# A transformer block on one core: order of the first columns, of the route and of the last experts' end

## The chip, the cores and the metric

The kernel runs on one core of a Trainium2 chip. The metric is device time in microseconds (us) of one execution; a kernel is compared by the median of several runs. The profile is that of one execution.

## The reference, cut to what matters

One block of a network on 256 tokens of width 2048, in float32:

```python
mod = silu(c) @ w_ada + b_ada                       # six vectors of 2048
sh1, sc1, gt1, sh2, sc2, gt2 = split(mod, 6)
h = rmsnorm(x, g_norm1) * (1 + sc1) + sh1
parts = split_cols(h @ w_in)                        # 10312 columns
y_att = dsa_attention(...)                          # indexer, top 64 keys, 8 heads
y_hg  = rmsnorm(hgrn2_recurrence(...), g_head) * silu(hog)
merged = sigmoid(ga) * (y_att @ w_attn_up) + sigmoid(gh) * (y_hg @ w_hgrn_up)
x = x + gt1 * (merged @ w_out)
h2 = rmsnorm(x, g_norm2) * (1 + sc2) + sh2
x = x + gt2 * hier_moe(h2, ...)                     # 4 groups of 8 experts, 2 experts a token
out = rmsnorm(x, g_final)
```

Each expert has a gate, an up (2048 x 512) and a down matrix (512 x 2048).

## The kernel before

**Stages.** Tokens lie in two tiles of 128 rows (t = 0, 1); the width is cut into KT = 16 slices j of 128. The stages run in the order of `Block.__init__`: `prepare`, `first_columns`, `middle_columns`, `merge`, `project` (which ends in `route`), `experts`, `overflow` (a branch that this input doesn't take) and `finish`.

**Weights.** All weights come over the SP queue. `unit` loads a piece of a dense matrix, `ada` a row block of w_ada (128 x 2048, 1 MB), both into a ring of RING = 5 slots of 1 MB. A ring slot is free again when its last reader is done, so SP waits at the first load whose slot isn't free, and everything behind it on that queue waits too.

**First columns.** The dense products up to w_out are made exact enough by splitting: `split_w` has ACT round a weight piece of two slices j to fp32r (`hi`, L249) and DVE subtract it (`lo`, L250), and `three` multiplies hi, lo and the low part of the left side in three matmuls (L273 to L275). `first_columns` takes the 16 slices in five groups (2, 3, 4, 4, 3 slices) and each group through 11 column blocks (9 of 512, 2 of 292). A group needs its normalized features (`features`: two ACT operations and one DVE subtraction per slice j), which need the two `ada` sums per slice, each one DVE instruction over 128 x 2048 (L388). In the first four groups the order on each engine is that of the program (`manual_schedule`): for a column block, its splits and matmuls (`column`), then the addition of the column block before (`add`: ACT copies in the first group, DVE adds later), then `ada` sums for the next group, and at the last column block `features` of the next group. `first_norm` makes the row norms and transposes x by 32 matmuls against a diagonal (eight pieces of four, each with one ACT copy, L348 and L350); `early` (the first sums and features) stands after the first two pieces. The fifth group and all until `project`'s end are ordered by the planner. `lower_bounds` and `router_weights`, called there, load small tensors over SP; the planner sends these loads far ahead.

**Project and route.** `tokens_out` adds the gate times the product to x, sums squares (ACT, L1018), transposes x on PE (L1021) and multiplies by the router weights (L1010). For the last quarter this and `route` stand in an order written out: `spread_rows` makes 128 equal rows of a quarter of the last gate by four matmuls (L431), `rows` copies them (L986). Then come the logits (L1050), the choice of experts on DVE, the positions by three matmuls (L1082 to L1084), `tokens_high` (ACT, L1030) and `tokens_low` (DVE, L1036).

**Experts.** 32 experts in pairs. `block(e, u)` multiplies one quarter of gate and up of expert e (2 MB of weights, L1185), with the tokens gathered by `gather` (L1367, L1370) four experts at a time; `hidden` makes silu(gate) * up; `down` multiplies a quarter of the down matrices of the pair (2 MB, L1293), scales by weight and gate (L1296), splits (L1298, L1299); `scatter` adds it to the tokens (L1380, L1381). The weights go through the order `ring_order`: 5 ring slots of 1 MB, one slot of 1 MB of tag t8 and R2 = 3 slots of 2 MB (`ring2`, whose memory is that of the closed dense pool). `slot` loads 1 MB (L1133), `two` 2 MB (L1144), or halves of a quarter (L1135, L1147).

**End.** At the last pair, `prepare_finish` takes two of the ring slots for the result (`zg`), resets the order to two ring slots and three of 2 MB, and makes the rows of g_final: per quarter four DVE scalings of the identity (L1389), one matmul (L1391) and two ACT copies (L1404). The last quarter of the down product is cut in two halves of 256 columns, each with loads of its own. `scale_columns` sums squares (L1413) and multiplies by g_final (L1416); `finish` makes the row factors (L1424 on), scales (L1429, L1430) and stores by eight DMAs (L1432).

## Time and profile before

| | |
|---|---|
| median of 3 runs | 1787.6 us (1783.95 to 1790.62) |
| profiled execution, its time | 1786.46 us |
| its span, first to last instruction | 1784.5 us |
| PE busy, DVE busy, ACT busy | 91%, 52%, 29% of the span |
| moved by DMA | 631.32 MB, mean 354 GB/s |

Spans are sums over stages with different limits, so the rows below are read stage by stage. In a row of a timeline the first number is the start, the second the duration or, for a merged row, the time from the first to the last end; the brackets give the idle time of that engine before it and what ended it. SPq is the queue on which SP issues DMAs; a number there is issue time, not transfer.

### The profile page before, as it was taken

Reading aid. Unit: us, or ns where it says so; the run is one execution under the profiler, and the core shown is the slowest. Engines: PE = TensorE matmul, PEld = TensorE weight load, DVE = VectorE, ACT = ScalarE, POOL = GpSimd, SP = SyncE. Lnnn points to the kernel's source line nnn. Section 1 sums busy time; section 2 is a strip of 40 time slices with the busy share of each in tenths; the row PEclk is TensorE's granted clock in tenths of the full one; section 3 lists DMA queues with packets and bytes.
Section 4 is the critical chain, followed back from the end, with each engine's and each line's share of the span. In section 5 each row is a group of like instructions: output and inputs, shape, how many; then the busy total and the mean of one; then the engine's idle time right before and its main releaser. Section 6 shows DMA issues by size and latency. Waiting matters only on the chain. (4 is left out here: it accounts for less than half of the span.)

```text
span 1784.5 us, 19070 instructions
## 1 busy us (share of the span) xinstructions
PE 1629.3 (91%) x7453; PEld 962.0 (54%) x7453; DVE 928.6 (52%) x1517; ACT 523.4 (29%) x876; POOL 8.5 (0%) x19
## 2 busy tenths in 40 slices
PE   4889998899999999999999998988989989889885
PEld 4667786577777888885343433433424334234232
DVE  5789798998788799763321222122212221232125
ACT  4533446365654444434020110200201102002003
POOL 0000000000000000000000000000000000000000
PEclk9999998899999999998999999999999999999998
DMA  8888765578667989887999999999999999999994
GB/s 309 304 329 325 254 232 187 218 262 310 260 239 294 342 328 353 333 300 322 423 425 424 425 424 425 423 426 424 424 424 425 424 424 423 425 424 425 424 409 179
DMA packets 82942, 631.32 MB, mean 354 GB/s; under 512 B 13120, under 2 KB 15456, under 8 KB 21920
## 3 DMA queue, kind: packets, MB, share of 16 engines
q1 hardware_dynamic: 81728, 627.04, 87.9%
q0 software_dynamic: 944, 2.94, 0.6%
q8 instruction: 61, 1.00, 0.2%
q14 instruction: 33, 0.27, 0.0%
q10 hardware_dynamic: 176, 0.07, 0.0%
HBM read 627.92 MB, written 2.10 MB: 353 GB/s over the span
## 5 line engine op out<-in xcount | busy, mean ns | idle before, releaser
L1185 PE MATMUL moe_acc<-moe_u,moe_xg 128*64 128x512 f32 x2048 | 479.4, 601 | 51.6 <-DMA moe_u<-w_exp_in 51.6
L1185 PEld LDWEIGHTS moe_acc<-moe_u,moe_xg 128*64 128x64 f32 x2048 | 153.7, 137 | 325.7 <-issue 248.0
L1293 PE MATMUL moe_acc<-moe_u,moe_hT 128*64 128x512 f32 (+1 forms) x1040 | 233.0, 590 | 18.4 <-DMA moe_u<-w_exp_down 17.7
L1246 DVE COPY moe_gu<-moe_acc 128x512 f32<-128x512 f32 x32 | 22.1, 691 | 330.3 <-PE moe_acc L1185 330.3
L1293 PEld LDWEIGHTS moe_acc<-moe_u,moe_hT 128*64 128x64 f32 x1040 | 81.1, 137 | 153.1 <-issue 136.0
L1296 DVE SCALAR_TENSOR_TENSOR moe_ys<-moe_acc,moe_cw,out_t 128x512 f32<-128x512 f32 (+1 forms) x65 | 48.3, 743 | 177.7 <-PE moe_acc L1293 177.6
L1298 ACT ACTIVATE moe_yp<-moe_ys 128x512 fp32r<-128x512 f32 (+1 forms) x65 | 40.5, 623 | 307.1 <-DVE moe_ys L1296 307.1
L274 PE MATMUL first_acc<-first_wl,first_t 128*128 128x512 f32 (+1 forms) x292 | 115.5, 395 | 13.3 <-DVE first_wl L250 13.1
L273 PE MATMUL first_acc<-first_wr,first_t 128*128 128x512 f32 (+1 forms) x292 | 113.8, 390 | 7.4 <-ACT first_wr L249 7.4
L275 PE MATMUL first_acc<-first_wr,first_t 128*128 128x512 f32 (+1 forms) x292 | 113.1, 387 | 0.0
L273 PE MATMUL gate_acc<-gate_wr,first_t 128*128 128x512 f32 x256 | 103.9, 407 | 0.7 <-ACT gate_wr L249 0.7
L249 ACT ACTIVATE first_wr<-first_u 128x1024 fp32r<-128x1024 f32 (+3 forms) x79 | 73.1, 932 | 101.8 <-PE first_acc L275 89.0
L274 PE MATMUL gate_acc<-gate_wl,first_t 128*128 128x512 f32 x256 | 102.4, 400 | 0.1
L275 PE MATMUL gate_acc<-gate_wr,first_t 128*128 128x512 f32 x256 | 102.1, 399 | 0.0
L1381 DVE TENSOR_TENSOR out_t<-out_t,moe_ps 128x512 f32<-128x512 f32 (+1 forms) x130 | 82.1, 673 | 31.9 <-PE moe_ps L1380 31.9
L250 DVE TENSOR_TENSOR first_wl<-first_u,first_wr 128x1024 fp32r<-128x1024 f32 (+3 forms) x79 | 81.9, 1067 | 25.8 <-ACT first_wr L249 25.6
L1257 ACT ACTIVATE moe_si<-moe_ps 128x256 f32<-128x256 f32 x32 | 12.4, 387 | 281.3 <-PE moe_ps L1254 281.3
L249 ACT ACTIVATE gate_wr<-gate_u 128x1024 fp32r<-128x1024 f32 x64 | 67.8, 1059 | 77.8 <-PE gate_acc L275 65.0
L250 DVE TENSOR_TENSOR gate_wl<-gate_u,gate_wr 128x1024 fp32r<-128x1024 f32 x64 | 77.7, 1221 | 18.2 <-ACT gate_wr L249 18.0
L1370 ACT ACTIVATE moe_xg<-moe_ps,pre_c,pre_c 128x256 f32<-128x256 f32 x128 | 63.7, 565 | 65.2 <-PE moe_ps L1367 64.5
L1380 PE MATMUL moe_ps<-moe_yp,moe_S 128*128 128x512 f32 (+1 forms) x260 | 77.8, 421 | 2.8 <-ACT moe_yp L1298 2.8
L1380 PEld LDWEIGHTS moe_ps<-moe_yp,moe_S 128*128 128x128 f32 x260 | 43.8, 188 | 60.3 <-issue 49.9
(366 smaller groups left out, 2359.1 us busy)
## 6 DMA issues: line engine op xcount, KB each, us to landing
moe_u<-w_exp_in SPq DMA_DIRECT2D x160, 1024.0 KB, 23.7
moe_u<-w_exp_in SPq DMA_DIRECT2D x48, 2048.0 KB, 24.7
moe_u<-w_exp_down SPq DMA_DIRECT2D x47, 2048.0 KB, 24.6
first_u<-w_ada SPq DMA_DIRECT2D x32, 1024.0 KB, 7.1
gate_u<-w_in SPq DMA_DIRECT2D x32, 1024.0 KB, 5.7
moe_u<-w_exp_down SPq DMA_DIRECT2D x32, 1024.0 KB, 24.2
gate_u<-w_ada SPq DMA_DIRECT2D x28, 1024.0 KB, 4.9
first_u<-w_in SPq DMA_DIRECT2D x18, 1024.0 KB, 7.0
```

Source lines behind the costliest of these rows:

```text
L249: nc.scalar.activation(hi, raw, AF.Copy)
L250: nc.vector.tensor_sub(lo, raw, hi.bitcast(F32))
L273: mm(out, lr, hi, start=start, stop=False)
L274: mm(out, lr, lo, start=False, stop=False)
L275: mm(out, ll, hi, start=False, stop=stop)
L1185: nc.tensor.matmul(gu[e][64 * k:64 * k + 64, :], xg[g][j][:, CAP * i:CAP * i + CAP], w[k][:, jj, :], start=j == 0, stop=j == KT - 1, skip_ ...
L1293: nc.tensor.matmul(yp[64 * i:64 * i + 64, :n], h[i][:, f, :], w[i][:, f, :], start=f == 0, stop=f == 3, skip_group_check=True)
L1296: nc.vector.scalar_tensor_tensor(raw, yp[:, :n], cw, self.gt2[:, c0:c0 + n], op0=OP.mult, op1=OP.mult)
L1298: nc.scalar.activation(ys[0], raw, AF.Copy)
L1370: nc.scalar.activation(x, ps[:, 0:n], AF.Identity, scale=self.mod[SC2][:, j:j + 1], bias=self.mod[SH2][:, j:j + 1])
L1380: self.nc.tensor.matmul(ps[:, :n], sc[:, t * 128:(t + 1) * 128], ys[i], start=i == 0, stop=i == 1)
L1381: self.nc.vector.tensor_add(self.z[t][:, s], self.z[t][:, s], ps[:, :n])
```

## The change

First columns: `first_norm` becomes a generator. Only its first two pieces come ahead of the first sums; the other six are spread over column blocks 1 to 6 of the first group. The splits of the next weight piece are put ahead of the matmuls of the present one (`parts`, `products`), and the first piece's ahead of the first features. The sums for the next group are spread over 9 instead of 10 column blocks, and the next group's features come in two lots, behind column blocks 5 and 9. The small loads (lower bounds, router weights and biases) move into the written-out order, behind the second column block of the second group.

Route: both tiles' transposes come ahead of the squares and router products; the gate's rows 0 to 2 come after the logits and `tokens_high(0)`, row block 3 after `tokens_high(1)`, which is behind the position matmuls. The squares' output goes to the gate's tile. In the experts' pool two small tags (`gu`, `si`, 6 KB per partition) are laid out first, which moves the three 2 MB slots up in the memory; the 512 B tile `grow` leaves the dense pool.

End: the rows of g_final are made at expert 21, one quarter behind each block, by `spread_rows` into one ring slot, which leaves the ring along with the t8 slot (10 MB instead of 12 MB from there). `zg` takes t8 slots. For the branch, x is put together in full at experts 28 and 29 by four DVE additions. The last down quarter is loaded whole, and its second half is scattered by one fp32 matmul per tile without the split. `finish` stores in three column blocks (512, 768, 768) instead of four.

```diff
+NORM_AT = 21
-    def first_norm(self, early):
+    def first_norm(self):
...
-            if g == 1:
-                early()
             for t in range(2):
...
+                if g or t:
+                    yield
+    def small_loads(self):
+        nc, a = self.nc, self.a
+        q = nc.sync
...
+        def parts(g, c):
+            (j0, nk), (c0, n) = groups[g], cols[c]
             for u0, m in pieces(j0, nk):
                 raw = self.unit(("w_in", u0, c0, n))
                 for q in range(0, m, 2):
                     hi, lo = self.split_w(raw[:, q:min(q + 2, m), :], n)
+                    yield hi, lo, u0 + q
...
+            norm = self.first_norm()
+            next(norm)
+            for sums in blocks:
+                sums()
+            G = scales(0, 0, groups[0][1])
+            work = ((g, c, part) for g in range(last) for c in range(len(cols)) for part in parts(g, c))
+            now = next(work)
+            features(0, 0, groups[0][1], G)
...
+            while now:
+                g, c, part = now
+                now = next(work, None)
+                products(g, c, acc, part)
+                if now and now[:2] == (g, c):
+                    continue
+                ahead, k = todo[g + 1], len(cols) - 2
+                if before:
+                    add(*before)
+                for block in ahead[len(ahead) * c // k:len(ahead) * (c + 1) // k]:
+                    self.ada(*block)()
+                half = groups[g + 1][1] // 2
+                if c == k // 2 + 1:
+                    features(g + 1, 0, half)
+                if c == k:
+                    features(g + 1, half, groups[g + 1][1])
+                if g == 1 and c == 1:
+                    self.small_loads()
+                if g == 0 and 1 <= c <= 6:
+                    next(norm, None)
...
         with self.tc.manual_schedule():
-            wide = [self.spread_rows(gate2[0], b) for b in range(2)]
             self.tokens_out(c, ps, gt, xs, ss, rt)
-            rows(0)
-            rows(1)
-            wide += [self.spread_rows(gate2[0], b) for b in range(2, 4)]
...
         self.tokens_high(0)
-        rows(2)
-        rows(3)
+        rows(0, 1, 2)
...
-        for c in range(1, 4):
+        self.tokens_high(1)
+        rows(3)
+        for c in range(2, 4):
             self.tokens_high(c)
...
+        self.mt([128, FF], "gu", 2), self.mt([128, 4, CAP], "si", 2)
...
+                    if e1 == NORM_AT:
+                        self.last_norm(u)
...
+    def last_norm(self, b):
+        if b == 0:
+            self.gf = self.big.tile([128, D], F32, name=self.name("gf"), tag="ring", bufs=RING)
+            n, i = len(self.ring_order), self.ring_i
+            self.ring_order = [self.ring_order[k % n] for k in range(i, i + n) if k % n not in (RING - 1, RING)]
+            self.ring_i = 0
+        ps = self.spread_rows(self.grow, b)
+        self.nc.scalar.activation(self.gf[:, 512 * b:512 * b + 512], ps, AF.Copy)
...
     def prepare_finish(self):
-        self.zg = [self.big.tile([128, D], F32, name=self.name("zg"), tag="ring", bufs=RING) for _ in range(2)]
-        self.ring_i, self.ring_order = 0, [("ring", self.big)] * 2 + [("ring2", self.moe)] * R2
...
+        self.zg = [self.t8([128, D]) for _ in range(2)]
+        self.ss = self.mt([128, 2, len(LAST_CHUNKS)], "ss", 1)
...
-        for c in range(4):
-            s = slice(512 * c, 512 * c + 512)
+        for c0, c1 in ((0, 512), (512, 1280), (1280, D)):
+            s = slice(c0, c1)
```

## Rows read from the trace of the kernel before

**Rows 1.** The page: GB/s in 40 slices; the largest matmul group.

```profile
GB/s 309 304 329 325 254 232 187 218 262 310 260 239 294 342 328 353 333 300 322 423 425 424 425 424 425 423 426 424 424 424 425 424 424 423 425 424 425 424 409 179
...
L1185 PE MATMUL moe_acc<-moe_u,moe_xg 128*64 128x512 f32 x2048 | 479.4, 601 | 51.6 <-DMA moe_u<-w_exp_in 51.6
```

**Rows 2.** Windows: length, busy PE, PEld, DVE, ACT, POOL (instructions), clock, DMA share, GB/s.

```profile
34.28:73.24 38.96, 33.52 (x133) 25.29 (x133) 27.09 (x30) 23.60 (x38) 0.00 (x0) 0.90 0.86 310
73.24:128.16 54.92, 46.70 (x199) 36.36 (x199) 48.85 (x66) 21.90 (x33) 0.00 (x0) 0.97 0.89 333
128.16:190.58 62.42, 59.27 (x265) 48.12 (x265) 55.67 (x68) 25.31 (x31) 0.00 (x0) 0.97 0.80 298
190.58:250.00 59.42, 57.13 (x256) 46.85 (x257) 50.92 (x62) 22.26 (x24) 0.00 (x0) 0.97 0.72 260
...
160.00:180.00 20.00, 20.00 (x87) 16.21 (x87) 19.82 (x22) 7.58 (x8) 0.00 (x0) 1.00 0.97 369
```

**Rows 3.** Timeline of the start: last scale, norm copies and matmuls, first product.

```profile
27.31 0.15 DVE L457 TENSOR_TENSOR first_sm<-pre_d,pre_c 128x2 f32<-128x2 f32 x1
...
29.45 2.53 ACT L350 ACTIVATE first_t<-first_ps 128x512 f32<-128x512 f32 x5
...
30.08 2.56 PE L348 MATMUL first_ps<-first_t,pre_t 128*128 128x128 f32 x16 [2.91 <-ACT first_t L350]
...
34.28 0.80 PE L273 MATMUL first_acc<-first_wr,first_t 128*128 128x512 f32 x1 [1.63 <-ACT first_wr L249]
```

**Rows 4.** Timeline at the end of the second group: features and next splits.

```profile
123.09 0.16 DVE L457 TENSOR_TENSOR first_sm<-pre_d,pre_c 128x4 f32<-128x4 f32 x1
...
127.06 2.94 ACT L249 ACTIVATE first_wr<-first_u 128x1024 fp32r<-128x1024 f32 x3
127.19 0.43 DVE L467 TENSOR_TENSOR first_t<-first_t,first_t 128x256 fp32r<-128x256 f32 x1 [0.52 <-ACT first_t L464]
128.14 1.23 DVE L250 TENSOR_TENSOR first_wl<-first_u,first_wr 128x1024 fp32r<-128x1024 f32 x1 [0.52 <-ACT first_wr L249]
```

**Rows 5.** Timeline of SP's queue: first and last of the small loads.

```profile
27.53 0.70 SPq L360 DMA_DIRECT2D lb_d<-hg_lower_bounds  x2
...
31.82 0.43 SPq L937 DMA_DIRECT2D lb_d<-b_router_expert  x1
```

**Rows 6.** Windows: while the small loads drain, and within the route.

```profile
30.00:32.00 2.00, 1.92 (x14) 1.92 (x15) 0.01 (x1) 1.98 (x5) 0.00 (x0) 0.86 0.95 88
...
808.00:810.00 2.00, 1.31 (x7) 0.91 (x6) 1.24 (x9) 1.51 (x4) 0.00 (x0) 0.50 0.00 0
```

**Rows 7.** Timeline of the route, to the first expert block.

```profile
802.61 2.05 PE L431 MATMUL out_acc<-out_t,pre_c 16*128 16x128 f32 x16
...
811.10 0.67 DVE L1050 SCALAR_TENSOR_TENSOR route_c<-out_ps,out_c,lb_d 128x32 f32<-128x32 f32 x4 [1.62 <-PE out_ps L1010]
...
814.80 1.31 SPq L1144 DMA_DIRECT2D moe_u<-w_exp_in  x3
...
815.25 0.64 PE L1082 MATMUL route_ps<-route_d,pre_d 128*128 128x32 f32 x2 [0.48 <-DVE route_d L1078]
...
815.30 3.77 ACT L1030 ACTIVATE out_t<-out_t,out_c 128x512 fp32r<-128x512 f32 x6
...
821.51 4.54 PE L1185 MATMUL moe_acc<-moe_u,moe_xg 128*64 128x512 f32 x16
```

**Rows 8.** Timeline of the end: g_final's rows, last down products, finish.

```profile
1741.79 1.65 DVE L1389 TENSOR_SCALAR moe_ys<-pre_c,lb_c 128x128 f32<-128x128 f32 x8
...
1746.85 7.09 PE L1293 MATMUL moe_acc<-moe_u,moe_hT 128*64 128x512 f32 x32
...
1767.19 0.48 DVE L1296 SCALAR_TENSOR_TENSOR moe_ys<-moe_acc,moe_cw,out_t 128x256 f32<-128x256 f32 x1
...
1771.93 0.22 DVE L1424 TENSOR_REDUCE fin_s<-moe_ss 128x1 f32<-128x5 f32 x2 [0.69 <-DVEq L1308]
...
1775.30 4.49 SPq L1432 DMA_DIRECT2D out<-moe_zg  x8
```

More of the change, by code (lines that the diff above doesn't have):

```diff
@@ L448, in first_columns, with scales, features @@
         todo = [[(part, j) for j in range(j0, j0 + nk) for part in (SC1, SH1)] for j0, nk in groups]
-        def features(g):
-            j0, nk = groups[g]
-            f = slice(j0, j0 + nk)
-            G = self.sm([128, nk, 2])
+        def scales(g, a, b):
+            j0 = groups[g][0]
+            f = slice(j0 + a, j0 + b)
+            G = self.sm([128, b - a, 2])
             nc.vector.tensor_add(G[:, :, 0], self.mod[SC1][:, f], self.bsc[:, f])
-            nc.vector.tensor_mul(G[:, :, 0], G[:, :, 0], self.cols[:, 96 + j0:96 + j0 + nk])
+            nc.vector.tensor_mul(G[:, :, 0], G[:, :, 0], self.cols[:, 96 + j0 + a:96 + j0 + b])
             nc.vector.tensor_add(G[:, :, 1], self.mod[SH1][:, f], self.cols[:, f])
+            return G
+        def features(g, a, b, G=None):
+            G = scales(g, a, b) if G is None else G
             rest = []
-            for i in range(nk):
-                j = j0 + i
+            for i in range(b - a):
+                j = groups[g][0] + a + i
                 h = self.t1([128, 256])
@@ L499, in first_columns @@
             blocks = [self.ada(*block) for block in todo[0]]
-            def early():
-                for sums in blocks:
-                    sums()
-                features(0)
             self.hr = [self.t8([128, 8, 256], F32R) for _ in range(2)]
@@ L1021, in tokens_out @@
                 nc.tensor.transpose(tp[t][:, i * 128:(i + 1) * 128], x2[t][:, i * 128:(i + 1) * 128], self.ident)
-            if t == 0:
-                router(0)
-        router(1)
+        for t in range(2):
+            nc.scalar.activation(self.gt2[:, 512 * t:512 * t + 512], x2[t], AF.Square, accum_out=ss[:, t, c:c + 1])
+            router(t)
     def tokens_high(self, c):
@@ L1189, in experts @@
         waiting = None
+        self.whole = []
         with self.tc.manual_schedule():
@@ L1317, in overflow @@
             self.ring_i, self.ring_order = 0, [("ring2", self.moe)] * R2
-            xg = self.gather(P, [], KT, [room[j // 8][:, j % 8, :] for j in range(KT)])
+            xg = [room[j // 8][:, j % 8, :] for j in range(KT)]
+            for j in range(KT):
+                ps = self.misc()
+                for t in range(2):
+                    nc.tensor.transpose(ps[:, t * 128:(t + 1) * 128], self.whole[t][:, j * 128:(j + 1) * 128], self.ident)
+                nc.scalar.activation(xg[j], ps[:, 0:256], AF.Identity, scale=self.mod[SC2][:, j:j + 1],
+                                     bias=self.mod[SH2][:, j:j + 1])
             win = self.win.rearrange("(q i) u p k j f -> q i u p k j f", i=2)
@@ L1378, in scatter @@
             ps = self.misc()
-            for i in range(2):
-                self.nc.tensor.matmul(ps[:, :n], sc[:, t * 128:(t + 1) * 128], ys[i], start=i == 0, stop=i == 1)
+            m = sc[:, t * 128:(t + 1) * 128]
+            for y in ys:
+                self.nc.tensor.matmul(ps[:, :n], m if len(ys) == 2 else m.bitcast(F32), y, start=y is ys[0], stop=y is ys[-1])
             self.nc.vector.tensor_add(self.z[t][:, s], self.z[t][:, s], ps[:, :n])
```

133 lines of the change are left out of this document (56 added, 77 removed).

## The prediction, made before the changed kernel was run

> **What bounds the kernel now.** I read the page's slices first, then windows, then timelines of the three places that the change touches. The GB/s slices [rows 1] show two kernels in one: from the twentieth slice on (about 850 us) the rate is flat at 424 GB/s and the largest matmul group waits 51.6 us for weights, so the experts are a weight stream that PE follows. Ahead of it the rate wanders between 187 and 353, and the engines set the pace. So the time is: when the stream can run freely, plus its length, plus what is left after its last byte. An engine saved inside the stream is worth nothing; time counts in the first columns (up to 250 us), in the route (802 to 826) and in the end (1740 on). Between 250 and 802 the instructions are the same; I assume that this stretch moves as a block.
>
> In the first columns the windows of the four written-out groups [rows 2] say which engine is full. At full clock 87 matmuls of 512 columns take 20.00 us, 0.23 each. A column block of 512 has 6 matmuls per slice, one of 292 costs 0.57 of that: a slice is 6 x (9 + 2 x 0.57) x 0.23 = 14.0 us of PE, so the groups of 2, 3, 4 and 4 slices need 28, 42, 56 and 56 us. They took 39.0, 54.9, 62.4 and 59.4 (the last is cut at 250). DVE is busy for 27.1, 48.9, 55.7 and 50.9 of these. So the first group is bound by neither (waits and a clock of 0.90), the second by DVE, the third by both, the fourth by PE.
>
> **First columns, start.** Before, the last scale factors are there at 27.46 (27.31 and 0.15), but the first product starts at 34.28 [rows 3]: on ACT the features are followed by five copies of the norm (29.45, 2.53) and one more, PE makes two late norm pieces (30.08, 2.56), and only then ACT makes the first split. With the split ahead, ACT has it done while DVE still sums, DVE's part (1.23, [rows 4]) follows the scales, and the first product can start at 27.46 + 1.23 = 28.7: 5.6 us earlier. But four of the pieces that PE made in its idle time before, and the two late ones, now lie between column blocks. A piece costs 1.28 at the low clock (30.08: two in 2.56) or about 1.03, by the gate's rows of the same number of matmuls (802.61: two in 2.05, [rows 7]); I take 1.1, six make 6.6. The first group is then 28 + 6.6, plus a cold start like before's (a clock of 0.90 over 39 us loses 3.9; I take 2.5, as there will be fewer gaps), plus 2 for waits: 39.1, from 28.7 to 67.8 instead of 73.24, **5.4 us earlier**. The waits were 7 us before (39.0 less 28 and 3.9); I cut them to 2 because each split is now a whole piece ahead of its matmuls, and because the small loads leave this group: while they drained, the DMA engines were 0.95 busy for 88 GB/s [rows 6].
>
> **Second to fourth group.** DVE is in order, and it can't split while it waits for the features. Before, the one lot of four took from 123.25 (123.09 and 0.16) to the next DVE split at 128.14, 4.9 us, of which four subtractions of 0.43 are work [rows 4]. ACT needs (127.06 - 123.25) / 4 = 0.95 per slice, then 1.08 to the split's DVE part. Two lots of two take 2 x (1.9 + 1.08) = 6.0: PE keeps a piece in stock across them, but DVE loses 1.1 more than with one lot. So the second group stays DVE's: 48.9 + 6.0 - 1.7 = 53.2 against 54.9, 1.7 gained. Against that stand the small loads: their issue takes 27.53 to 32.25 on SP, 4.7 us [rows 5], and queued behind them are the weights of the next column blocks, for which DVE and PE wait. Before, SP had nothing to issue there, as its slots were not free; now it has, with a DMA share of 0.89 [rows 2]. The cost is between 0 (five slots in stock) and 4.7; I take 1.5, as most of the stock covers it: **0.2 gained**. Third group: DVE 55.7 + 6.0 - 1.7 = 60.0 is over PE's 56; 62.4 - 60.0 = 2.4, less 1.0 because two engines that are both nearly full don't mesh: **1.4**. Fourth group: lots of one and two slices, DVE 50.9 + 5.0 - 1.3 = 54.6, so PE's 56 binds; 59.4 less 56 is 3.4, of which I take **2.0**. Together 5.4 + 0.2 + 1.4 + 2.0 = **9.0**. Bounds: 2 (small loads 4.7, waits in the first group as before, nothing else gained) and 15 (no waits at all).
>
> **Route.** Here the change moves two things that pull against each other. The weights first: DMA stands at 0.00 in the middle of the route at half clock [rows 6], until three loads of 2 MB are issued at 814.80 [rows 7], just when PE's last gate rows (they read a tile of the dense pool) are over. By the order in which the pools lay out their tags, the first 2 MB slot lies over that tile; with 6 KB more ahead of it and 512 B less below, it lies over the split buffers, free at 802.6. So the 8 us hole should go. But the ring is full after these 6.3 MB (14.8 us at 424): before, the stream had them at 814.8 + 14.8 = 829.6, and the first block was released at 826.05 (821.51 and 4.54), so it went on at once. Now they are there by about 821, and the next load waits for that release. Of the 3.5 us between 826.05 and 829.6 a part is lost again, as expert 0's blocks each have a gather and release slower than the stream; I take 1 as gained.
>
> Then the release itself. The two gate blocks that stood ahead of the transposes (2.05 at 802.61) go, so the logits (811.10) come about 2 us earlier, 809.1; from logits to positions DVE takes 4.15 (815.25). But three gate blocks now stand on PE between them: at the half clock that [rows 6] shows, 2 us each, 809.1 + 6.1 = 815.2: nothing is won. The fourth stands ahead of the gather, and behind its copy wait four of six `tokens_high` (3.77 for six, so 2.5) and with them the copies of the gathered tokens, which before began at 819.07. I take the first block 1 us later. Sum of the route: **0**; bounds 2 lost and 5 gained.
>
> On the clock a page speaks against this order: the Trainium skill, "TensorE: Matmul & The Clock Gate", section "HAM oscillation — how this bites in real kernels", says that idle gaps of PE bring the slow clock back. This trace agrees (0.50 at 808 to 810), and by that rule the low clock would come sooner here, since the two gate blocks filled PE right behind the product: the 16 router matmuls would be slowed too, by up to the 2.05 that 16 such matmuls cost at full clock. The route would then lose 2 instead of 0 and the time be 1773.6; with no fall of the clock at all it is rival B.
>
> **End.** The g_final work goes from the end to expert 21, where PE waits for weights in every pair [rows 1] and covers four matmul blocks; without that cover it would cost 4 us. From the first DVE scaling (1741.79) to the first down product (1746.85) are 5.06 us [rows 8] in which PE could have started: gone. The slice before the last moved 409 instead of 424 GB/s [rows 1], 15/424 x 44.6 = 1.6 us of stream lost when the result took ring slots: gone, as PE waits for those weights. From 1746.85 to the last scaling at 1767.19 PE and DVE keep their chain. The last half saves an ACT copy and a DVE subtraction, and pays for fp32 matmuls: 0.9 either way, I take 0.3 gained. Eight stores in 4.49 are 0.56 each; two fewer save 1.1, larger last ones give part of it back: 0.4. The last quarter now lands whole: the last slice has 179 x 44.6 = 8.0 MB, less 2.1 of output 5.9 MB, 13.9 us from 1740, so at about 1752.2, and PE wants it at 1740.2 + 3 x 3.55 and two scatters: up to 1 us of wait, I take 0.4. Sum 5.1 + 1.6 + 0.3 + 0.4 - 0.4 = **7.0**, bounds 4 and 9.
>
> **Sum.** 9.0 + 0 + 7.0 = 16.0 us. Against the profiled execution's own 1786.46 (span 1784.5 and 2.0 around it) that is 1770.5; that execution lies 1.1 below the median of the runs, so the forecast for the median is 1787.6 - 16.0 = **1771.6**.
>
> **Rivals.** (A) DVE and DMA give the first columns' gain back: the norm's pieces and the small loads fall on engines with no slack, the first part gives 1 and only the end is left: 1787.6 - 8 = 1779.6. For it: DVE busy 48.9 of 54.9, DMA share 0.89. Against it: the first group, where most of the gain is, has DVE busy for only 27.1 of 39.0. (B) Everything meshes: 13 in the first columns, PE at the full clock in the route for 4 (gate blocks of 1.03 take 3.1 and hide behind DVE's choice), 7 in the end: 1787.6 - 24 = 1763.6. Against it: the 0.50 clock. (C) Slower: from expert 21 the ring has 10.5 MB instead of 12.6. With one block in use 8.4 MB are queued, 19.8 us at 424. If PE ever holds blocks longer than that behind their landing, the stream stops for a block (4.95 us) in each pair; 5.5 pairs cost 27: 1771.6 + 27 = 1798.6. Against it: PE waits for weights through the whole stretch, so it is near the stream's head, not 19.8 us behind. (D) The hole stays, because the 2 MB slots still lie over tiles that the gate rows hold, now read later: the stream starts up to 4 us later: 1775.6, within the forecast's own range.
>
> **Chances and range.** The forecast with D inside it 0.63, A 0.18, B 0.15, C 0.04. What 0.5% is worth here, 9 us, is about what a measurement of this kernel can tell from no change; so faster means under 1778.7. Of the forecast nearly all lies there, of A a good third, B all: 0.81. Same: the rest of A and a little of the forecast, 0.14. Slower: C and an unlucky new order of the planner between 250 and 802, 0.05. The range from 1762 to 1780 takes in the forecast, B and most of A: the sum of lower bounds (2 - 2 + 4) and upper bounds (15 + 5 + 9) is wider, but they won't fall together.
>
> **What would show it.** In the profile after: the first product near 28.7 and the second group near 68; no stretch of 4.9 without a DVE split at group ends, but two of about 3 per group at the lots; small loads near 80 us; the 2 MB loads issued near 803 in the route's own time and DMA idle near 821 instead; clock 0.50 there; expert 21 with gate-like matmuls and no loss of GB/s; the first down product of the last pair within 1 us of `hidden`; the reduce of `finish` about 7 us nearer to the last expert block. Wrong would be a first group of over 44 us, a DVE wait for weights behind the small loads of over 4, or GB/s under 420 after expert 21.

## The result and the profile after

The changed kernel takes 1778.0 us, the median of 7 runs from 1775.3 to 1779.4; the kernel before takes 1787.6 (1784.0 to 1790.6). The ratio is 0.9948, with a 95% interval from 0.9939 to 0.9957: 9.3 us faster, where 16.0 were forecast. The profiled execution took 1776.45 (span 1774.5), 10.0 less than that of before.

The page after, GB/s in 40 slices and the largest matmul group, beside [rows 1]:

```profile
GB/s 335 299 316 324 288 209 222 258 242 277 235 251 293 340 342 341 332 306 343 420 425 422 424 422 424 422 423 424 422 424 421 425 424 423 424 424 424 424 423 214
...
L1214 PE MATMUL moe_acc<-moe_u,moe_xg 128*64 128x512 f32 x2048 | 477.8, 599 | 46.8 <-DMA moe_u<-w_exp_in 46.3
```

It is still two kernels in one. The stream runs at 424 from the same slice on, the dip to 409 ahead of the last slice is gone, and PE waits 46.3 us for weights instead of 51.6. So the gain must lie at the stream's two ends.

The start, as a timeline (columns as in [rows 3]):

```profile
26.58 0.15 DVE L467 TENSOR_TENSOR first_sm<-pre_d,pre_c 128x2 f32<-128x2 f32 x1
26.65 1.22 DVE L252 TENSOR_TENSOR first_wl<-first_u,first_wr 128x1024 fp32r<-128x1024 f32 x1
...
27.93 0.80 PE L275 MATMUL first_acc<-first_wr,first_t 128*128 128x512 f32 x1 [6.11 <-ACT first_t L479]
```

The split follows the last scale at once and the first product stands at 27.93 instead of 34.28. The four written-out groups as windows, beside [rows 2]. A group's start is found by counting products (6 per slice and column block). The fourth window runs on to the second column block of the fifth group, and the last line is the same stretch before:

```profile
27.93:68.56 40.63, 38.52 (x180) 31.67 (x180) 27.46 (x34) 26.06 (x45) 0.00 (x0) 0.96 0.86 303
68.56:125.84 57.28, 48.50 (x199) 35.87 (x199) 49.97 (x69) 23.65 (x35) 0.00 (x0) 0.97 0.88 316
125.84:188.96 63.12, 59.48 (x265) 48.06 (x266) 56.67 (x72) 24.46 (x30) 0.00 (x0) 0.97 0.82 306
188.96:254.06 65.10, 63.22 (x283) 51.32 (x282) 56.69 (x82) 27.34 (x33) 0.00 (x0) 0.97 0.68 246
...
190.58:256.12 65.54, 63.25 (x283) 51.70 (x283) 56.39 (x76) 28.12 (x34) 0.00 (x0) 0.97 0.68 248
```

The first group ends at 68.56 instead of 73.24, 4.7 us sooner; the second at 125.84 instead of 128.16, only 2.3 sooner; the third at 188.96 instead of 190.58, 1.6 sooner. The first block of 292 columns stands once in each group; its times, and those of later milestones, before and after:

| milestone | before | after | difference |
|---|---|---|---|
| first product | 34.28 | 27.93 | -6.4 |
| end of the first group | 73.24 | 68.56 | -4.7 |
| block of 292 in group 2 | 87.38 | 81.77 | -5.6 |
| in group 3 | 147.63 | 142.65 | -5.0 |
| in group 4 | 210.00 | 205.68 | -4.3 |
| second column block of group 5 | 256.12 | 254.06 | -2.1 |
| end of the last w_out product | 802.68 | 798.78 | -3.9 |
| first expert block | 821.51 | 816.00 | -5.5 |
| last expert block (31, 3) | 1735.91 | 1732.12 | -3.8 |
| reduce of `finish` | 1771.93 | 1762.58 | -9.4 |
| end of the span | 1784.5 | 1774.5 | -10.0 |

The early start and the first group give 4.7 us. In the next three, where 3.6 more were to be gained, 2.6 are lost: 2.4 in the second and 0.7 in the third, and 0.4 come back in the fourth. PE's idle time in these three (length less busy time) was 13.7 us before and is 14.3 after, so the new order moved the stalls of PE and didn't remove them. The longest of them stand at the lots. The timeline of the first lot of the third group, DVE and PE, to be read against [rows 4]:

```profile
155.43 2.29 DVE L398 CUSTOM_DVE_ANT_0 first_u<-first_u,pre_d 128x2048 f32<-128x2048 f32 x1
...
157.91 0.15 DVE L467 TENSOR_TENSOR first_sm<-pre_d,pre_c 128x2 f32<-128x2 f32 x1
159.19 0.42 DVE L482 TENSOR_TENSOR first_t<-first_t,first_t 128x256 fp32r<-128x256 f32 x1 [1.12 <-ACT first_t L479]
160.12 0.43 DVE L482 TENSOR_TENSOR first_t<-first_t,first_t 128x256 fp32r<-128x256 f32 x1 [0.51 <-ACT first_t L479]
161.07 2.36 DVE L252 TENSOR_TENSOR first_wl<-first_u,first_wr 128x1024 fp32r<-128x1024 f32 x2 [0.52 <-ACT first_wr L251]
...
161.09 0.50 PE L275 MATMUL first_acc<-first_wr,first_t 128*128 128x512 f32 x1 [1.77 <-ACT first_wr L251]
162.35 0.62 PE L276 MATMUL first_acc<-first_wl,first_t 128*128 128x512 f32 x1 [0.76 <-DVE first_wl L252]
```

DVE makes the scales, then waits 1.12 for ACT, does 0.42, waits 0.51, does 0.43, and waits 0.52 for the next split's first half, which ACT makes behind the features. PE's stock doesn't last: it stands still for 1.77 and 0.76. And the granted clock falls behind that stall (windows of 2 us, same columns as above, the clock third from the right):

```profile
160.00:162.00 2.00, 0.50 (x1) 0.19 (x1) 1.36 (x2) 2.00 (x4) 0.00 (x0) 1.00 0.85 311
162.00:164.00 2.00, 1.65 (x4) 1.30 (x5) 2.00 (x4) 0.93 (x1) 0.00 (x0) 0.65 0.99 369
164.00:166.00 2.00, 2.00 (x6) 1.57 (x5) 2.00 (x3) 0.00 (x0) 0.00 (x0) 0.50 0.84 315
```

0.50 is the lower of the two levels, 1.2 of 2.4 GHz. Windows of 2 us from 24 to 256 show four such dips after, each behind a stall of PE: those near 57, 163 and 225 at a lot, that near 91 at the splits for the blocks of 292. The clock lost is 6.8 us in all (the sum of 2 us times what is missing to 1.00); before it was 10.2, of which 3.4 at the start and the rest in four dips behind it. A stall doesn't always bring a dip: PE also stood for 1.95 at the lot at 101.22, and the clock stayed at 1.00.

The route and the memory, as a timeline, beside [rows 7]:

```profile
799.18 4.56 SPq L1174 DMA_DIRECT2D moe_u<-w_exp_in  x3
803.27 4.58 PE L441 MATMUL route_acc<-out_t,pre_c 16*128 16x128 f32 x24
808.87 0.63 PE L1111 MATMUL route_ps<-route_d,pre_d 128*128 128x32 f32 x2 [1.02 <-DVE route_d L1107]
...
810.28 2.07 PE L441 MATMUL route_acc<-out_t,pre_c 16*128 16x128 f32 x8
812.28 3.78 PE L1407 MATMUL moe_ps<-moe_P,out_t 128*128 128x256 f32 x16
816.00 4.60 PE L1214 MATMUL moe_acc<-moe_u,moe_xg 128*64 128x512 f32 x16
...
820.62 6.50 SPq L1164 DMA_DIRECT2D moe_u<-w_exp_in  x4
```

The 2 MB loads go out at 799.18 instead of 814.80, and the next load only at 820.62, when the first block gives its slots back. The stream's idle stretch has moved behind the loads (windows of 8 us; last two columns the DMA share and GB/s):

```profile
800.00:808.00 8.00, 7.24 (x47) 6.66 (x45) 6.24 (x32) 4.57 (x11) 0.00 (x0) 0.77 0.99 400
808.00:816.00 8.00, 7.13 (x31) 6.62 (x31) 7.08 (x19) 5.31 (x10) 0.00 (x0) 0.50 1.01 429
816.00:824.00 8.00, 8.00 (x41) 3.81 (x42) 0.56 (x3) 3.25 (x7) 0.00 (x0) 0.88 0.49 174
```

The end, as a timeline, beside [rows 8]:

```profile
1732.12 3.65 PE L1214 MATMUL moe_acc<-moe_u,moe_xg 128*64 128x512 f32 x14 [1.33 <-DMA moe_u<-w_exp_in]
1737.14 4.65 PE L1331 MATMUL moe_acc<-moe_u,moe_hT 128*64 128x512 f32 x16
...
1758.75 0.48 DVE L1334 SCALAR_TENSOR_TENSOR moe_ys<-moe_acc,moe_cw,out_t 128x256 f32<-128x256 f32 x1
1759.29 1.40 PE L1421 MATMUL moe_ps<-moe_ys,moe_S 128*128 128x256 f32 x4 [1.86 <-DVE moe_ys L1334]
1762.58 0.16 DVE L1463 TENSOR_REDUCE fin_s<-moe_ss 128x2 f32<-128x10 f32 x1 [0.68 <-DVEq L1348]
1765.88 3.71 SPq L1471 DMA_DIRECT2D out<-moe_t  x6
```

From the last expert block to the end it is 42.4 us; before it was 48.6.

### The profile page after: what moved, and what is told of

Read it like the earlier page. It is cut to its first block, busy times and chain, and to the rows that moved or that the text cites. A ratio compares the mean times of both kernels' runs of the same rounds, so it can differ in the third digit from the quotient of the medians.

```text
span 1774.5 us, 19069 instructions
## 1 busy us (share of the span) xinstructions
PE 1630.5 (92%) x7476; PEld 959.9 (54%) x7476; DVE 929.7 (52%) x1507; ACT 519.9 (29%) x868; POOL 8.5 (0%) x19
## 5 line engine op out<-in xcount | busy, mean ns | idle before, releaser
L1214 PE MATMUL moe_acc<-moe_u,moe_xg 128*64 128x512 f32 x2048 | 477.8, 599 | 46.8 <-DMA moe_u<-w_exp_in 46.3
L1331 PE MATMUL moe_acc<-moe_u,moe_hT 128*64 128x512 f32 (+1 forms) x1040 | 237.2, 590 | 20.6 <-DMA moe_u<-w_exp_down 19.6
L1338 ACT ACTIVATE moe_yp<-moe_ys 128x512 fp32r<-128x512 f32 x64 | 40.1, 627 | 311.8 <-DVE moe_ys L1334 311.8
L251 ACT ACTIVATE gate_wr<-gate_u 128x1024 fp32r<-128x1024 f32 x64 | 67.8, 1059 | 78.4 <-PE gate_acc L277 67.2
L275 PEld LDWEIGHTS first_acc<-first_wr,first_t 128*128 128x128 f32 x292 | 57.1, 196 | 32.5 <-ACT first_wr L251 6.7
```

Of the source, the lines that this page charges most:

```text
L251: nc.scalar.activation(hi, raw, AF.Copy)
L275: mm(out, lr, hi, start=start, stop=False)
L1214: nc.tensor.matmul(gu[e][64 * k:64 * k + 64, :], xg[g][j][:, CAP * i:CAP * i + CAP], w[k][:, jj, :], start=j == 0, stop=j == KT - 1, skip_ ...
L1331: nc.tensor.matmul(yp[64 * i:64 * i + 64, :n], h[i][:, f, :], w[i][:, f, :], start=f == 0, stop=f == 3, skip_group_check=True)
L1338: nc.scalar.activation(ys[0], raw, AF.Copy)
```

## Experiments

Each run is held against the kernel before, run on the same chip beside it (medians 1786.8, 1786.6 and 1786.0 in the three series). Differences are told in us of 1787, from the ratios. The changed kernel, run once more in the third series, gave 0.9950, so 0.9949 stands for it; a ratio's interval is about 2.5 us to either side, and a difference to the changed kernel is known to about 3, so that differences of 2 us can't be told from nothing, and the traces must help.

**First columns as before.** Everything else as changed.

```diff
-            norm = self.first_norm()
-            next(norm)
...
-            now = next(work)
-            features(0, 0, groups[0][1], G)
+            self.first_norm(early)
...
+                    acc = column(g, c)
...
+                    if c == len(cols) - 1:
+                        features(g + 1)
```

> The changed kernel with the first columns, their norm and the small loads as they were before (features in one lot at the end of a group, all transposes first, no split ahead); route, memory and end stay as changed. Theory: the first columns are worth only what reaches the last product of w_out, where the two traces differ by 3.9 us (802.3 and 798.4), so this kernel is 4 us slower than the changed one (3 to 5.5) and the other parts keep about 6 of the 10 us. Rival (the forecast): the nine us of the first columns are real and the other parts gave less than forecast; then it is 7 to 9 us slower. In its trace the first product stands at about 34.3 and the last product of w_out near 802 under both; what differs is where the hog accumulation begins: near 309 if the first columns carry their whole gain that far, and the gate columns begin within 2 us of the changed kernel's 374 if the middle stage gives it back.

1778.2 us, ratio 0.9962 (0.9948 to 0.9975): 2.3 us slower than the changed kernel, which is inside the noise. In its trace the first product stands at 34.80, 6.9 later, and the end of the last w_out product at 801.44, 2.7 later. So of the forecast's nine us some 2.5 are there, less than even the theory's 3 to 5.5. The two signs decide nothing, as the planner orders the stretch behind the groups differently in the two kernels: the hog accumulation begins at 308.03 here and at 300.33 in the changed kernel, the gate columns at 371.04 and 374.33. But the giving back is done ahead of that stretch: the second column block of group 5 stands at 254.28, against 254.06. The other 2.4 of the 2.7 us arise behind it, where traces with the same code differ as much (see the last section). Counted from the first product to that block, it is 219.5 here and 221.8 in the kernel before, and from 225.0 to 226.8 in the five traces that have the new order with all else (the two of the changed kernel and the three that follow). **From the first product on the new order is 3 to 7 us slower**, and that is most of the 6 us by which it starts sooner. The six norm pieces alone, which the old order has ahead of the first product, are 6.3 us of PE in it; so splits ahead and two lots, on the whole, brought the groups nothing yet.

**Route in the old order.**

```diff
         with self.tc.manual_schedule():
+            wide = [self.spread_rows(gate2[0], b) for b in range(2)]
             self.tokens_out(c, ps, gt, xs, ss, rt)
+            rows(0)
+            rows(1)
+            wide += [self.spread_rows(gate2[0], b) for b in range(2, 4)]
...
-        rows(0, 1, 2)
+        rows(2)
+        rows(3)
...
```

> The changed kernel with the order from the last product to the first gather as before (the gate rows' four blocks ahead of the logits, the router's products of one half ahead of the other half's transposes). Theory: the new order brings the first expert block 1.6 to 2.5 us nearer to the last product of w_out (18.9 us behind it before, 17.3 changed), the stream waits for that block's slots, so this kernel is 1.5 to 2.5 us slower. Rival (the forecast): the block moves but the stream sets the time and the order is worth nothing, within 0.5 us of the changed kernel.

1779.1, ratio 0.9959 (0.9945 to 0.9973): 1.8 slower, which is inside the noise. The trace says less: from the end of the last w_out product to the first expert block it is 17.5 us here and 17.2 in the changed kernel. The order alone is worth 0.3, so the theory's 1.6 falls and the forecast's "0" for the order stands.

**Memory as before.**

```diff
-        self.mt([128, FF], "gu", 2), self.mt([128, 4, CAP], "si", 2)
```

> The changed kernel without the two lines' worth of early allocation of gu and si ahead of the ring's 2 MB slots, nothing else. Theory: the two 2 MB loads are again issued only when the route ends (before: 814.80, changed: 799.18 and 802.45), the transfer engines stand idle near 808 instead of 816 to 824, and since either way the ring is refilled only by the release of the first expert block, the time moves by the data that the early loads carry ahead: 4 MB less ahead is at most 10 us of stream, less the idle stretch of 816 to 824 that vanishes with it, so 1 to 3 us slower. Rival: the early loads are worth the full hole, 4 us and more. Other rival: nothing (within 0.5), as the ring is as full at the first release either way.

1781.2, ratio 0.9969 (0.9958 to 0.9981): 3.6 slower, between the theory's 1 to 3 and the first rival. The 2 MB loads go out at 814.27, and the idle stretch stands where it stood in the kernel before:

```profile
800.00:808.00 8.00, 6.90 (x36) 6.63 (x37) 6.34 (x30) 4.41 (x9) 0.00 (x0) 0.66 0.39 133
808.00:816.00 8.00, 8.00 (x36) 7.49 (x35) 5.89 (x19) 4.24 (x9) 0.00 (x0) 0.50 0.17 32
816.00:824.00 8.00, 8.00 (x40) 4.60 (x39) 2.44 (x6) 4.06 (x9) 0.00 (x0) 0.78 0.94 397
```

In the 24 us it moves 4.5 MB where the changed kernel moves 8.0. The gain shows in the stream: from the first expert block to the last one it is 919.5 here and from 914.9 to 916.1 in the eleven traces with the new memory and the new end. From the last w_out product to the first block it is 18.3 instead of 17.2, with the same order of instructions on PE, but that is no effect of the layout: two traces with the new memory, of the runs with norm pieces ahead and with both below, have 18.3 and 18.2 too. What goes with it is how early the clock falls in the route. The 16 router products, here in the run with norm pieces ahead and in the changed kernel:

```profile
800.24 3.18 PE L1044 MATMUL out_ps<-first_d,out_t 128*128 128x36 f32 x16
...
801.41 1.93 PE L1041 MATMUL out_ps<-first_d,out_t 128*128 128x36 f32 x16
```

So the layout is worth about 3.6, by way of the stream.

**End as before.** The last norm's rows in `prepare_finish`, the ring cut to two slots there, the last quarter in halves with their own loads, split and two products, four stores.

```diff
-                    if e1 == NORM_AT:
-                        self.last_norm(u)
...
     def prepare_finish(self):
-        self.zg = [self.t8([128, D]) for _ in range(2)]
+        self.zg = [self.big.tile([128, D], F32, name=self.name("zg"), tag="ring", bufs=RING) for _ in range(2)]
+        self.ring_i, self.ring_order = 0, [("ring", self.big)] * 2 + [("ring2", self.moe)] * R2
...
+            ps = self.rows_of(self.gfin[:, 4 * c:4 * c + 4])
```

> The changed kernel with the end as before: the last norm's rows made behind the last expert in prepare_finish, ring cut to two slots there, last down block in halves with their own loads, split raw and two products, one scale for each 256 columns, four stores of 512 columns. Theory: the end is worth what it measured between the traces from the last block's matmuls to the end, 6 to 7.6 us, so this kernel is 6 to 7.5 us slower than the changed one. Rival: the end was worth less alone, 4 us, because the dip of the stream near the last experts belongs to the ring's state and not to the cut. In its trace the first down product of the last pair begins about 5 us behind the last hidden, in the changed kernel within 0.1 us.

1782.6, ratio 0.9975 (0.9966 to 0.9984): 4.6 slower, below the theory. The timeline of its end:

```profile
1731.28 3.65 PE L1221 MATMUL moe_acc<-moe_u,moe_xg 128*64 128x512 f32 x14 [1.27 <-DMA moe_u<-w_exp_in]
...
1737.16 1.65 DVE L1425 TENSOR_SCALAR moe_ys<-pre_c,lb_c 128x128 f32<-128x128 f32 x8
...
1743.88 7.09 PE L1329 MATMUL moe_acc<-moe_u,moe_hT 128*64 128x512 f32 x32
...
1768.96 0.22 DVE L1460 TENSOR_REDUCE fin_s<-moe_ss 128x1 f32<-128x5 f32 x2 [0.68 <-DVEq L1344]
```

From the last block to the reduce it is 37.7 us, in the changed kernel 30.5: 7.2 less, near the 7 of the forecast (in the kernel before it was 36.0). But from the first expert block to the last one it is 913.5 here and 916.1 changed, and 914.9 to 915.9 in the ten other traces with the new end and the new memory. The stream reaches the last block 1.5 to 2.6 us later with the new end, which doesn't cut the ring at the last pair. That fits loads of the last down blocks that are let go sooner and share the engines with the blocks ahead of them; it is argued, not shown. With the 0.7 that is saved behind the reduce the end is worth 5.3 by the trace.

**Features in one lot.**

```diff
-                if c == k // 2 + 1:
-                    features(g + 1, 0, half)
                 if c == k:
-                    features(g + 1, half, groups[g + 1][1])
+                    features(g + 1, 0, groups[g + 1][1])
```

> The changed kernel with a group's features in one lot (where the second lot stands), all else as changed. Theory: a lot costs VectorE its wait for ScalarE (1.12 us for the first feature and 0.52 for each further one, in the lots of both kernels), two lots pay the first wait twice, so splitting the lot hides nothing: within 1 us of the changed kernel, rather below, and VectorE's waits for the features' line fall from 10.2 to near 7.5 us between 66 and 250. Rival (the forecast's step): two lots are hidden behind the queue of split weights and one is not, so one lot brings back some 1.5 us of idle TensorE at each of the three later group ends, 3 to 5 us slower.

1773.5, ratio 0.9918 (0.9905 to 0.9932): 5.5 faster. The rival, which is the forecast's step, falls: two lots are not better hidden than one. DVE's waits between 66 and 250, what waits, for whom, and us, times and longest; the changed kernel first:

```profile
DVE first_wl L252 <- ACT first_wr L251: 13.4, 20, 2.1
DVE first_t L482 <- ACT first_t L479: 10.2, 12, 1.1
```

and with one lot:

```profile
DVE first_wl L252 <- ACT first_wr L251: 15.2, 18, 2.8
DVE first_t L482 <- ACT first_t L479: 7.8, 12, 1.1
```

The waits for the features fall from 10.2 to 7.8, as the theory has it, but those for the split's first half rise, and the sum is nearly the same. Its profiled execution is the longest of its five (1776.6), and its groups take 224.8 from the first product, 1 us less than the changed ones. So 1 us is seen in the trace, as the theory has it; where the rest of the 5.5 lies is open, and by its median the theory's "within 1 us" failed.

**Scales ahead of the adds.** The three small DVE steps that make a lot's scales go ahead of the column's add and sums; the subtractions stay.

```diff
+                half = groups[g + 1][1] // 2
+                lot = {k // 2 + 1: (0, half), k: (half, groups[g + 1][1])}.get(c)
+                G = scales(g + 1, *lot) if lot else None
                 if before:
                     add(*before)
...
+                if lot:
+                    features(g + 1, *lot, G)
```

> The changed kernel with the three small VectorE steps that make a lot's scales moved ahead of the column's adds and sums, so that ScalarE can make the features while VectorE still adds; the subtractions stay where they are. Theory: what eats the first columns' gain is VectorE waiting for ScalarE at each lot (10.2 us in total between 66 and 250) and TensorE behind it (about 2.5 us a lot at 101, 161 and 222); with the scales early these waits go, the column of 292 of the fifth group comes 4 to 6 us sooner after the first product than the changed kernel's 235.2, and the time falls by 3 to 6 us. Rival: in the second group VectorE is busy 49 of 57 us and in the third and fourth TensorE over 56 of 61; the waits are only where the slack shows, and the time stays within 1 us.

1765.8, ratio 0.9883 (0.9868 to 0.9899): **11.8 us faster** than the changed kernel, twice the theory. Its waits of DVE between 66 and 250:

```profile
DVE first_wl L252 <- ACT first_wr L251: 10.6, 17, 1.6
DVE first_t L482 <- ACT first_t L479: 1.0, 2, 0.5
```

and the timeline of the same lot:

```profile
149.01 0.15 DVE L467 TENSOR_TENSOR first_sm<-pre_d,pre_c 128x2 f32<-128x2 f32 x1
...
149.81 2.28 DVE L398 CUSTOM_DVE_ANT_0 first_u<-first_u,pre_d 128x2048 f32<-128x2048 f32 x1
...
152.03 0.76 DVE L482 TENSOR_TENSOR first_t<-first_t,first_t 128x256 fp32r<-128x256 f32 x2
152.70 2.35 DVE L252 TENSOR_TENSOR first_wl<-first_u,first_wr 128x1024 fp32r<-128x1024 f32 x2
```

From the end of the sums to the next split DVE needs 0.7 instead of 3.4 (157.64 to 161.07), since ACT made the features meanwhile. The waits for features and for splits fall by 12.0 in all. From the first product to the second column block of group 5, the changed kernel first:

```profile
27.93:254.06 226.13, 209.74 (x924) 166.92 (x925) 190.79 (x254) 101.51 (x141) 0.00 (x0) 0.97 0.80 291
27.80:241.13 213.33, 202.37 (x924) 161.18 (x925) 189.92 (x254) 101.84 (x141) 0.00 (x0) 1.00 0.84 310
```

That is 213.3 instead of 226.1, and PE's idle time falls from 16.4 to 11.0. The other 7 us are the clock, for the same products: no window of 2 us between 24 and 256 is below 0.95, where the changed kernel lost 6.8. So a lot's stall can be paid twice, once standing and once at half speed. Not all of the 6.8 is owed to the lots: the waits at the blocks of 292 stand in this trace too (0.78 and 0.98, at 81.58 and 86.03) and brought no dip here, and the profiled execution is the fastest of its four, 2.5 under their median. The four traces with the scales ahead in the new order lost 0, 0, 1.7 and 3.4 us of clock, the five with the changed first columns 6.8 to 11.9.

**Norm pieces ahead of the first product.** Four of the six.

```diff
             norm = self.first_norm()
-            next(norm)
+            for _ in range(3):
+                next(norm)
...
             now = next(work)
+            for _ in range(2):
+                next(norm)
```

> The changed kernel with four of the six norm pieces (eight transposes and one copy each, 1.05 us of TensorE) that stand between the first group's columns moved ahead of the first product, where TensorE waits 6.1 us for ScalarE. Theory: the first group of the changed kernel is bound by TensorE (36.2 of 38.1 us busy), so the first group ends 3 to 4 us sooner if the first product stays near 27.9, and later if ScalarE's copies (0.6 us each) delay it; the gain arrives at the end of w_out in part: 1 to 3 us faster. Rival: VectorE's splits and sums set the first group's length, and nothing is gained (within 0.7).

1774.7, ratio 0.9928 (0.9914 to 0.9941): 3.8 faster. The first product stays at 27.72 and the block of 292 of the second group comes at 78.91 instead of 81.77; the pieces fit into PE's wait of 6.11. The first group ends at 65.75 instead of 68.56, 2.8 sooner, a little under the theory's 3 to 4 (its "36.2 of 38.1" is of a window that ends 2.6 us ahead of the group's end; to the end it is 38.5 of 40.6).

**Both.** The two edits together.

> Both: scales ahead of the adds, and four norm pieces ahead of the first product. Theory: different stretches, so the gains add: 4 to 9 us faster than the changed kernel, near 1770. Rival: the second group is bound by VectorE and takes from either what it gives, so that both together give no more than the larger of the two alone.

1761.9, ratio 0.9856 (0.9841 to 0.9871): 16.6 faster, and 11.8 and 3.8 make 15.6. The gains add, so neither takes the other's cover.

**The changed kernel again.**

> The changed kernel once more, beside the three below: what the other runs are held against. Theory: 1775 to 1778 and 0.994 to 0.995 of the kernel before. If it lies nearer to 1774, the gain that one lot showed (ratio 0.9918) is for the most part the difference of two measurements.

1776.5, ratio 0.9950 (0.9935 to 0.9964), as the theory has it; so the gain of one lot is not the difference of two measurements of the changed kernel.

**Old first columns with scales ahead.** The edit of the scales alone, on the old order (one lot, transposes first, no split ahead).

```diff
                     acc = column(g, c)
+                    G = scales(g + 1) if c == len(cols) - 1 else None
                     if before:
...
-                        features(g + 1)
+                        features(g + 1, G)
```

> The first columns as before the change (no splits ahead, one lot of features at a group's end, transposes first), but with the three small VectorE steps for the scales moved ahead of the last column's adds; route, memory and end as changed. Theory: VectorE's wait for the features goes here too (7.7 us between 66 and 250 in the same kernel without the move), but the split weights that stand behind the lot still come late, so it is 3 to 7 us faster than the first columns as before (1778.2 in the first series), and slower than the scales' move in the changed order (1765.8). Rival: the move alone gives all, 1766 to 1769, and splits ahead and two lots are worth only the first product's few us.

1774.1, ratio 0.9931 (0.9918 to 0.9945): 5.5 faster than the first columns as before, and 8.6 slower than the scales ahead in the new order. DVE's wait for the features only falls from 7.7 to 5.5 there; that it would go was wrong, since the one lot of four needs more of ACT's time than the add covers (no sums stand in a group's last column). So with the scales ahead the new order is worth 8.6 us, and without them 2.3, which is inside the noise. **The forecast's nine us are in the change, but behind a stall that it kept.**

**Scales and norm ahead, one lot.**

```diff
-                lot = {k // 2 + 1: (0, half), k: (half, groups[g + 1][1])}.get(c)
+                lot = (0, groups[g + 1][1]) if c == k else None
```

> Scales ahead and four norm pieces ahead, with the features in one lot. Theory: with the scales early a lot no longer stalls VectorE, so the number of lots doesn't matter: within 1.5 us of both together (1761.9, ratio 0.9856). Rival: two lots now hide better, one lot is 2 to 4 us slower.

1766.8, ratio 0.9890 (0.9875 to 0.9906): 6.1 slower than both with two lots; the theory falls, its rival stands, by more than its 2 to 4. DVE waits 3.4 for features instead of 1.0, and 11.5 instead of 9.6 for splits: with up to four features in one lot ACT needs longer than the add that now covers it (no sums stand in that column), and its trace lost 3.4 us of clock where that of both lost none. Two lots pay once the scales are ahead.

**Last gate block out of the route.** On top of both.

```diff
+            kept = self.gt2[0:16, 1536:1664]
+            nc.gpsimd.tensor_copy(kept, gate2[0])
...
-        self.tokens_high(1)
-        rows(3)
+        self.row3 = lambda: rows(3)
...
+                    if e1 == 1 and u == 3:
+                        self.row3()
```

> Scales ahead, norm pieces ahead, and the last of the four blocks of gate rows taken out of the route: it is made behind the second expert's last block, from a copy of its rows that GpSimd makes. Theory: in the route the block takes TensorE from 810.28 to 812.36 at half clock just ahead of the gather, but the gather's own choices are ready only at 811.64, so the first expert block comes 0.6 us sooner and the time moves by no more: within 0.7 us of both together. Rival: the whole 2.1 us go, and with the slots' release that much of the time.

1759.0, ratio 0.9854 (0.9835 to 0.9873), the same as both within the noise, as the theory has it. From the last w_out product to the first block it is 16.3 in its trace, and 17.2 with the block in place where the router products took 1.93: 0.9 sooner, near the theory's 0.6 and not the rival's 2.1. It is the fastest kernel here, 26 us under the one before.

## Why the forecast was right in places and 7 us too good

- **First columns, start: right.** The first product was put at 28.7 and stands at 27.93; the group's end at 67.8 and stands at 68.56, 4.7 us gained for 5.4. The six norm pieces in the columns were priced rightly (6.3 for 6.6) and still cost what could be had for nothing, 3.8.
- **Second to fourth group: the failed step.** The forecast gave them 0.2, 1.4 and 2.0, 3.6 in all, and they gave -2.4, -0.7 and 0.4, a loss of 2.6. It had the two stretches of 3 us a lot, but said that PE "keeps a piece in stock across them". PE ran dry at 161.09 and at other lots, and the term had no clock in it: three lots, one of them in the first group, were followed by a dip, and a dip takes some 1.7 us more. The clock's price was counted for the start and weighed for the route only, while the fourth group was priced at PE's 56 us of full clock. There a reading was off too: the 59.4 are of a window cut at 250, and the old group's products run to 251.93, 61.4 us. With the stall removed the second column block of group 5 begins at 241.13, 15.0 before the old kernel's 256.12, and the forecast's 9.0 would have been too low.
- **Small loads: cost too high.** They were issued from 64 to 72 and DVE waited 0.2 us for data between 66 and 250; 1.5 was booked.
- **Route: right in sum, for other reasons.** The order is worth 0.3 by the trace. The first block came 1.6 sooner, not 1 later, from the last product on: three gate blocks took 4.58 and not 6.1, as the clock fell to 0.50 only behind 804, and were over ahead of the positions. Where it fell sooner, in three traces of the new order, the block came only 0.5 to 0.6 sooner than before. The rule of the Trainium skill that was weighed there ("TensorE: Matmul & The Clock Gate", section "HAM oscillation — how this bites in real kernels": idle gaps bring the slow clock back) would have cost 2 us in the route. Three of the twelve traces with the new order show about half of that loss (router products of 3.1 to 3.2 us, first block 18.2 to 18.3 us behind the last product), eight show none of it (1.93 and 17.2), and the twelfth, with one gate block less, shows none either (1.93). At the lots, where the rule was not applied, the trace agrees with it: 0.50 behind the stall at 161.09.
- **Memory: undersized.** The hole went and the idle stretch moved behind the loads, as forecast, but what is left is 3.6 and not 1, for the most part as a stream that reaches the last block sooner. The case D had priced the hole at 4.
- **End: mechanism right, 2.4 too much.** PE's side gave 7.2 to the reduce. The dip of 1.6 was credited as stream gained, yet the last block doesn't come sooner for it: 914.4 us behind the first block before and 916.1 after (914.9 to 915.9 in the other traces). The rows of g_final run at 1423.2 to 1438.8 and cost no GB/s; case C didn't happen. The landing of the last quarter was put at 1752.2, where 1740 and 13.9 make 1753.9; it bears on a term of 0.4 only.
- **Sum.** By single runs: 2.3 first columns, 1.8 order, 3.6 memory, 4.6 end, which is 12.3 for the 9.1 measured; the 3 us between lie within the noise of four differences. The parts need not add either: with the old end, the stream from first to last block is 914.4 with the old memory and 913.5 with the new, with the new end 919.5 and 916.1. Case A came nearest (1779.6), and by luck for the most part: its norm pieces cost what the forecast had booked, its small loads next to nothing, and it had the end at 7 and no gain from the memory. Right in it is only that DVE, in order, gave gain back. That 1778.0 lies in the range and under the 1778.7 that was to count as faster is luck too: it is 0.7 us, and the forecast's own parts were off by more.

## What to carry over

Where an engine works in order and feeds another, look for a chain that goes out to a third engine and comes back (scales, features, subtractions): start it one step ahead of work that can cover it, and only then think about how the work is cut into lots. Price a stall of TensorE by what the clock takes behind it as well as by its own length. And when a gain fades stage by stage, count from the first product: what is lost then shows per group, apart from where the kernel began.

## What the runs showed of the hardware

- A stall of TensorE of 1.8 and 0.8 us (161.09, 162.35) was followed by a fall of the granted clock to 0.50 for some 3 us, in the middle of a stretch otherwise near full; with the stalls at the lots gone the clock stayed at 1.00 for over 200 us in two of four traces and lost 1.7 and 3.4 us in the others. A stall of 1.95 at 101.22 brought no fall; one of 1.97 at the same place in the run with the end as before (103.03) did. What decides between them is open.
- In the route the same order of instructions on PE got the clock's fall sooner or later from trace to trace: the 16 router products took 1.93 us in nine traces and 3.10 to 3.18 in three, one with the old memory layout and two with the new.
- The stretch from the second column block of group 5 to the last w_out product took 544.7 us in some traces (changed, end as before) and 546.8 to 547.2 in others (route as before, memory as before), with no edit of the code there. From 300 to 376 the granted clock was 0.90 and 0.91 in the first two, and 0.88 and 0.86 in the others. What sets it is open.
